# Down products of the first four inner tiles of the second feed-forward stage as products of halves

## The chip, the core and the metric

The kernel runs on one core of a Trainium2 chip. The time is that of the device, in microseconds (us), from the start of the program to its end on that core. The engines have names that the profile shortens: PE (TensorE, matrix products), PEld (its weight loads, beside PE), DVE (VectorE), ACT (ScalarE), POOL (GpSimd), SP (SyncE, which here only issues DMAs). SBUF is the on-chip memory, PSUM the accumulators that PE writes.

## The reference, cut to what matters

One decoder layer over 512 tokens of width 1024, all in 32-bit floats:

```python
def swiglu_ffn(x, g, w_gate, w_up, w_down):
    h = rms_norm(x, g)
    return (jax.nn.silu(h @ w_gate) * (h @ w_up)) @ w_down
...
x = x + 0.5 * swiglu_ffn(x, ffn1_norm, ffn1_w_gate, ffn1_w_up, ffn1_w_down)
...
x = x + 0.5 * swiglu_ffn(x, ffn2_norm, ffn2_w_gate, ffn2_w_up, ffn2_w_down)
```

Between the two lie two attention branches, which the change doesn't touch. The inner width of a feed-forward stage is 2816, which is 22 inner tiles of 128 (numbered f, from 0).

## The kernel before

**Layout.** x lies in SBUF as eight tiles of 128 features by 512 tokens (`x[d]`, all in one tile `gx`, which `xa` views). Products are computed with features on the partitions and tokens along the columns.

**Three products for one.** A 32-bit operand is split into a high part (rounded to the type that PE takes in one pass, `fp32r`) and a low part, the remainder. `mm3` (lines 155 to 157) issues high x high, low x high and high x low. The weights are split by `split_w` in the kernel: ACT casts the raw tile to `wh` (line 123), and DVE subtracts for `wl` (line 130), or, with `adding`, ACT negates and a DMA of POOL that adds in memory does the rest. `wh` and `wl` have three buffers each, so a step's weights can be split up to two steps ahead.

**Products of halves.** A product of two matrices cut in 2 x 2 blocks needs eight products of blocks; a known scheme (Strassen's, in Winograd's form) needs seven, with sums of blocks ahead of them and behind. The kernel uses it for most of a feed-forward stage. Tokens are cut in halves of 256 (`HT`). Of the weights, blocks A, B, C, D are loaded, and the sums S1 = C + D, S2 = S1 - A in the signs used, S2 + B and C + A are formed. Of the activations, the moving operands are `b1` and `b2` (halves as they are) and the sums `ta` and `tb`, each with high and low part. The order of the seven steps is 1, 5, 6, 2, 7, 3, 4, with moving operands b1 first half, ta first, tb first, b2 first, ta second, b2 second, tb second.

**Stages of `ffn(n, nxt)`.** `GROUPS` cuts the 22 inner tiles into (0,4), (4,10), (10,16), (16,22). In the first group everything is plain: for each of the four inner tiles a gate and an up step (24 products of 512 columns each, over the eight x tiles), then `activate` (DVE multiplies by the norm scale `rb`, ACT applies Silu, DVE multiplies gate and up; `split_act` splits the result); then eight down steps, one for each output tile d, by `run_down`, each with 12 products of 512 columns (four inner tiles, three terms). The first two put their last inner tile off behind both. In the other three groups the gate and up products of each pair of inner tiles are seven steps of halves (`pair_steps`, 24 products of 256 columns a step), and the down products of the group are two sets `s` of seven steps (`halved_steps(lo, s)`, each set for four output tiles, `GK` = 3 pairs, so 18 products of 256 columns a step).

**Beside the first group** of the second stage, `combine(k)` forms the operands of halves of x for the pair steps, for k of 0 to 3: the normalised x in a tile `xn` in buffer `rd` (line 336), then the sums (lines 340 to 343) and the splits (lines 328 and 329). Two pieces of it are emitted behind each step as soon as the norm scale is there, and behind the last one `rd` becomes free for raw weights.

**Order.** PE runs in program order throughout. `look_ahead(i)` splits the weights of step i and the next two, and issues loads up to six steps ahead while one of the raw buffers `ra`, `rb`, `rc`, `re`, `rf` (and later `rd`) is free; all these loads go through SP's queue. From `ordered[0]`, the first pair step, ACT, DVE and POOL also run in program order; ahead of it a scheduler orders them when the program is built, by program order as a priority and by its own estimate of when things are ready. On the chip that order is fixed.

Of the kernel before, what the change touches and what calls it, by code (L numbers as in the profile page):

```python
# [12 lines left out]
F32 = mybir.dt.float32  # L13
F32R = mybir.dt.float32r
AF = mybir.ActivationFunctionType
OP = mybir.AluOpType
# [32 lines left out]
HK = KD // 2  # L49
GK = 3  # L50
HALVED = (4, 10, 16)
FIRST = [0, 1, 4, 5, 2, 3, 6, 7]


@with_exitstack
def tile_hybrid_layer(ctx: ExitStack, tc: tile.TileContext, a: dict):
# [14 lines left out]
    def tmp_tile(name):  # L71
        return tmp.tile([P, T], F32, tag="t", name=name)
# [31 lines left out]
    def stream(i, dtype, name):  # L104

        return xpool.tile([P, 2 * T], dtype, tag=f"X{i}", name=name)
# [101 lines left out]
    def ffn(n, nxt):  # L208
# [3 lines left out]
        with tc.tile_pool(name=f"ffn{n}", bufs=1) as ap, tc.tile_pool(name=f"halves{n}", bufs=1) as hp:  # L212
# [21 lines left out]
            def halves(q):  # L234
                lo = next(lo for lo, hi in GROUPS if lo <= 2 * q < hi)
                j = q - lo // 2
                if q not in act:
                    tiles = [ap.tile([P, 2 * T], F32R, tag=f"a{j}{i}", name=f"a{i}") for i in "hl"]
                    ta = stream(6 + j, F32R, "ta") if j < 2 else ap.tile([P, 2 * T], F32R, tag="a2t", name="ta")
                    b1 = ap.tile([P, T], F32R, tag=f"a{j}b", name="b1")  # L240
                    act[q] = dict(b2=[t[:, :T] for t in tiles], tb=[t[:, T:] for t in tiles],
                                  ta=[ta[:, :T], ta[:, T:]], b1=[b1[:, :HT], b1[:, HT:]])
# [62 lines left out]
            def activate(f, pg, pu, rb):  # L305
                g = tmp_tile("g")
                V.tensor_mul(g, pg, rb)
                S.activation(g, g, AF.Silu)
                u = tmp_tile("u")
                V.tensor_mul(u, pu, rb)  # L310
                V.tensor_mul(u, u, g)
                split_act(f, u, 1 < f < PLAIN - 1)


            def parts_tile(nm, cols):
# [183 lines left out]
            def halved_steps(lo, s):  # L499

                t, raw = {}, {}
                n_w = 2 * GK * P
                end = lo + 2 * GK == KF
                direct = end and s and n == 2
                to_mix = end and n == 1

                def split(src, between=None):
                    return split_w(src, n_w, halves=True, between=between)
# [2 lines left out]
                    return lambda: V.tensor_add(dst[:, :n_w], x0[:, :n_w], x1[:, :n_w])  # L511

                def split_a():
                    t["s1"] = stream(0, F32, "s1")
                    return split(raw["a"][0], add(t["s1"], raw["c"][0], raw["d"][0]))

                def split_s1():
                    t["s2"] = stream(1, F32, "s2")
                    w = split(t["s1"], add(t["s2"], t["s1"], raw["a"][0]))
                    G.dma_start(raw["c"][0][:, :n_w], raw["a"][0][:, :n_w], accum_op=OP.add)  # L520
                    return w

# [1 line left out]
                    add(t["s2"], t["s2"], raw["b"][0])()  # L524

                def split_b():
                    if s:
                        return split(raw["b"][0], add_b)
                    w = split(raw["b"][0], late.pop("fa"))
                    late.pop("b2")()  # L530
                    add_b()
                    return w

                def split_s4():
                    if s:
# [7 lines left out]
                    return ps.rearrange("p (m t) -> p m t", m=2)  # L543

                def product(nm, w, b, half, start, each=None):
                    wh, wl = (z[:, :n_w].rearrange("p (m k c) -> p m k c", m=2, k=GK) for z in w)
                    order = [(m, k) for ks in (range(GK - 1), [GK - 1]) for m in range(2) for k in ks]
                    if each:
                        order.sort()
                    for i, (m, k) in enumerate(order):  # L550
                        h, l = (z[:, half * HT:half * HT + HT] for z in act[lo // 2 + k][b])
                        mm3(t[nm if each is None else nm + "01"[m]][:, m * HT:(m + 1) * HT], wh[:, m, k], wl[:, m, k], h, l,
                            start and i == 0, i == 2 * GK - 1 or (each is not None and k == GK - 1), skip_group_check=True)
                        if each and k == GK - 1:
                            each(m)

                def add_up(nm, part, half, done, sign=0.5, ms=(0, 1)):
# [67 lines left out]
                def run_4(w):  # L625
# [9 lines left out]
                return [Step(raw, [load["c"], load["d"], load["a"]], split_a, run_1),  # L635
                        Step(raw, [], split_s1, run_5),
                        Step(raw, [load["b"]], lambda: split(t["s2"]), run_6, "a"),
                        Step(raw, [], split_b, run_2, "b"),
                        Step(raw, [], lambda: split(raw["c"][0]), run_7, "c"),
                        Step(raw, [], split_s4, run_3),  # L640
                        Step(raw, [], lambda: split(raw["d"][0]), run_4, "d")]

            def run_down(d, lo, hi, held={}):

# [85 lines left out]
            def load():  # L730
                i, (key, f, src) = queue.pop(0)

                tag = max(sorted(free), key=lambda z: used[::-1].index(z) if z in used else len(used))
                free.remove(tag)
                used.append(tag)
                t = ap.tile([P, 1024], F32, tag=tag, name=tag) if tag in ("rd", "re", "rf") else raw_tile(tag)
                steps[i].raw[key] = t, tag
                nc.sync.dma_start(t[:, :f * P].rearrange("p (n m) -> p n m", n=f) if f else t, src)

            def look_ahead(i):  # L740

# [725 lines left out]
def _layout(x, ffn1_norm, ffn1_w_gate, ffn1_w_up, ffn1_w_down, mix_norm, w_in, b_forget,  # L1467
# [8 lines left out]
    for n, (g, u, dn) in ((1, (ffn1_w_gate, ffn1_w_up, ffn1_w_down)), (2, (ffn2_w_gate, ffn2_w_up, ffn2_w_down))):  # L1476
# [5 lines left out]
        o[f"w_down{n}"] = _fm(dn)  # L1482

        dh = _fm(dn)[:, :, PLAIN:].reshape(2, 2, 2, P, -1, GK, 2, P)
        o[f"w_halves{n}"] = dh.transpose(4, 1, 0, 6, 3, 2, 5, 7).reshape(-1, 2, 4, P, 2 * GK, P)
    c = lambda lo, hi: w_in[:, lo:hi]
    o["w_s"] = _tm(np.concatenate([c(2056, 2120), c(2696, 2760), c(2120, 2184), c(1536, 1544), c(2760, 2768)], axis=1))[:, FIRST]
# [32 lines left out]
```

## Time and profile before

| what | value |
|---|---|
| median of 3 runs | 1048.84 us (1047.35 to 1049.34) |
| the profiled execution, whole | 1048.76 us |
| its span | 1047.0 us |
| gate and up steps of the first group, second stage | about 719 to 763.4 us |
| its eight down steps | 763.4 to 785.1 us |
| pair steps and halved down steps behind it | 785.1 to 1047.0 us |

The span is the time between the first and the last record of the profiled execution; the rest of its own time lies around it. How to read the rows of the timeline: start in us, duration in us, engine, line of the kernel, operation, out<-in by the program's names, shapes, a count where equal instructions are merged, and in brackets the time that the engine sat idle before it with what ended that. The duration of an instruction is from its start to its end; instructions of one engine overlap a little, so the pace of a row of them is read from start to start.

DVE's work by stage, from the windows view (start and end, length; busy us and number of instructions of PE, PEld, DVE, ACT, POOL; granted TensorE clock; DMA share; GB/s):

```profile
719.00:763.40 44.40, 44.40 (x204) 36.86 (x203) 30.24 (x55) 25.07 (x38) 5.44 (x6) 1.00 0.46 107
763.40:785.10 21.70, 21.70 (x97) 17.98 (x96) 18.55 (x27) 7.54 (x12) 0.00 (x0) 1.00 0.55 175
785.10:804.00 18.90, 18.90 (x167) 18.88 (x166) 12.95 (x13) 9.87 (x12) 0.00 (x0) 1.00 0.29 93
```

### The profile page before, as it was taken

The page shows a single profiled execution, that of the slowest core. Times are in us where ns is not written, and L with a number is a line of the kernel's source. Part 1 is how long each engine was busy: PE and PEld are TensorE (multiplying, and loading weights), DVE is VectorE, ACT ScalarE, POOL GpSimd, SP SyncE. Part 2 cuts the span into 40 slices and gives each one's busy share as a digit, 9 for nine tenths or more (in the row PEclk, how much of TensorE's full clock was granted, in tenths as well). Part 3 has the DMA queues.
Part 4 walks back from the last instruction along what each step waited for, and adds up shares of the span by engine and source line. Part 5 has one row for each costly group of instructions (what it writes and reads, how often), then busy time and mean ns, then how long its engine had stood idle before and what let it go on. Part 6 is the DMA issues. An engine that isn't in the chain of part 4 may idle for free.

```text
span 1047.0 us, 19507 instructions
## 1 busy us (share of the span) xinstructions
PE 1036.7 (99%) x7438; PEld 965.7 (92%) x7438; DVE 852.4 (81%) x1402; ACT 669.0 (64%) x1118; POOL 257.7 (25%) x323
## 2 busy tenths in 40 slices
PE   9999999999999999999999999999999999999998
PEld 7889999999999899999977788888889999999998
DVE  6897888897989689977777865854887888988887
ACT  6547765865777765577867665443735865775773
POOL 1100111120121025286876653000100210111111
PEclk9999999999999999999999999999999999999999
DMA  7444764666567367633324321432553666567554
GB/s 256 107 151 122 156 165 131 149 164 172 120 149 181 87 149 182 197 98 95 92 66 120 118 71 51 154 132 77 129 168 91 151 148 182 126 161 189 135 127 131
DMA packets 57341, 142.66 MB, mean 136 GB/s; under 512 B 6424, under 2 KB 15768, under 8 KB 57248
## 3 DMA queue, kind: packets, MB, share of 16 engines
q1 hardware_dynamic: 39600, 110.21, 34.3%
q0 software_dynamic: 17504, 30.94, 16.5%
q8 instruction: 58, 0.95, 0.4%
q10 hardware_dynamic: 144, 0.27, 0.1%
q14 instruction: 35, 0.29, 0.1%
HBM read 104.94 MB, written 3.42 MB: 103 GB/s over the span
## 4 chain that ended last, share of the span: by engine, by line
PE 69%; DVE 3%; POOL 2%; issue 2%; ACT 1%; DMA 0%; POOLq 0%; ACTq 0%; DVEq 0%
PE pB L155 3%; PE pB L157 3%; PE pB L156 3%; PE ps_f L155 3%; PE ps_f L157 3%; PE ps_f L156 3%; PE ps_t L157 3%; PE ps_t L155 3%; PE ps_t L156 3%; PE pA L155 2%; PE pA L156 2%; PE pA L157 2%; PE dB L155 2%; PE dB L157 2%; PE dB L156 2%
## 5 line engine op out<-in xcount | busy, mean ns | idle before, releaser
L123 ACT CAST wh<-s 128x1024 fp32r<-128x1024 f32 (+1 forms) x90 | 86.7, 964 | 65.7 <-PE pC L156 31.6
L130 DVE TENSOR_TENSOR wl<-s,wh 128x1024 fp32r<-128x1024 f32 (+1 forms) x90 | 100.3, 1114 | 19.9 <-ACT wh L123 19.6
L155 PE MATMUL ps_t<-wh,xh 128*128 128x256 f32 (+1 forms) x288 | 81.9, 284 | 0.0
L157 PE MATMUL ps_t<-wh,xl 128*128 128x256 f32 (+1 forms) x288 | 81.2, 282 | 0.2 <-DVE xl L168 0.2
L156 PE MATMUL ps_t<-wl,xh 128*128 128x256 f32 (+1 forms) x288 | 81.0, 281 | 0.0
L155 PE MATMUL pB<-tbh,wh 128*128 128x256 f32 x288 | 79.5, 276 | 0.0
L156 PE MATMUL pB<-tbl,wh 128*128 128x256 f32 x288 | 79.5, 276 | 0.0
L157 PE MATMUL pB<-tbh,wl 128*128 128x256 f32 x288 | 79.5, 276 | 0.0
L249 POOL DMA_DIRECT2D b<-gu x12 | 10.4, 863 | 220.4 <-DVE rb L449 89.4
L155 PE MATMUL ps_f<-xh,wh 128*128 128x512 f32 x152 | 60.8, 400 | 0.0
L157 PE MATMUL ps_f<-xh,wl 128*128 128x512 f32 x152 | 59.6, 392 | 0.0
L156 PE MATMUL ps_f<-xl,wh 128*128 128x512 f32 x152 | 59.5, 392 | 0.0
L155 PEld LDWEIGHTS ps_t<-wh,xh 128*128 128x128 f32 x288 | 54.8, 190 | 0.4
L156 PEld LDWEIGHTS ps_t<-wl,xh 128*128 128x128 f32 x288 | 54.7, 190 | 0.4
L157 PEld LDWEIGHTS ps_t<-wh,xl 128*128 128x128 f32 x288 | 54.6, 190 | 0.4 <-DVE xl L168 0.4
L1237 ACT ACTIVATE p<-p,mn 128x512 f32<-128x512 f32 (+1 forms) x64 | 35.9, 561 | 28.5 <-DVE mn L1235 28.2
L157 PEld LDWEIGHTS pB<-tbh,wl 128*128 128x128 f32 x288 | 54.1, 188 | 0.0
L156 PEld LDWEIGHTS pB<-tbl,wh 128*128 128x128 f32 x288 | 54.1, 188 | 0.0
L155 PEld LDWEIGHTS pB<-tbh,wh 128*128 128x128 f32 x288 | 54.1, 188 | 0.0
L575 POOL DMA_DIRECT2D gx<-e x20 | 23.9, 1241 | 119.9 <-ACT wh L123 100.4
L1239 POOL TENSOR_SCALAR p<-p,rs 128x512 f32<-128x512 f32 (+1 forms) x64 | 39.6, 622 | 54.5 <-DVE rs L1238 50.3
L1251 DVE TENSOR_TENSOR pl<-pt,ph 128x512 fp32r<-128x512 f32 (+1 forms) x64 | 31.0, 485 | 19.4 <-ACT ph L1250 19.3
(404 smaller groups left out, 4195.3 us busy)
## 6 DMA issues: line engine op xcount, KB each, us to landing
rf<-in_w_pair_dram SPq DMA_DIRECT2D x15, 512.0 KB, 4.1
rc<-in_w_pair_dram SPq DMA_DIRECT2D x12, 512.0 KB, 3.5
re<-in_w_pair_dram SPq DMA_DIRECT2D x12, 512.0 KB, 3.7
rd<-in_w_pair_dram SPq DMA_DIRECT2D x12, 512.0 KB, 3.9
rb<-in_w_pair_dram SPq DMA_DIRECT2D x12, 512.0 KB, 4.2
gx<-e POOLq DMA_DIRECT2D x22, 256.0 KB, 4.3
ra<-in_w_pair_dram SPq DMA_DIRECT2D x9, 512.0 KB, 3.6
rd<-in_w_halves_dram SPq DMA_DIRECT2D x12, 384.0 KB, 3.8
```

The lines of the kernel that those rows point to most:

```text
L123: S.copy(wh[:, :f], raw[:, :f])
L130: V.tensor_sub(wl[:, :f], raw[:, :f], wh[:, :f].bitcast(F32))
L155: PE.matmul(out, lh, rh, start=start, stop=False, **more)
L156: PE.matmul(out, lh, rl, start=False, stop=False, **more)
L157: PE.matmul(out, ll, rh, start=False, stop=stop, **more)
L249: G.dma_start(l, src, accum_op=OP.add)
L575: G.dma_start(xa[:, d:d + 2, HT:], t["e"][part], accum_op=OP.add)
L1237: S.activation(p, p, AF.Exp, bias=mn, scale=-1.0, accum_out=rs)
L1239: G.tensor_scalar(p, p, rs, 1.0, op0=OP.mult, op1=OP.mult)
L1251: V.tensor_sub(pl[:, sl], pt[:, sl], ph[:, sl].bitcast(F32))
```

## The change

In the second stage alone (`FRONT = (2,)`) the eight plain down steps of the first group become two sets of `halved_steps(0, s)`, with two pairs of inner tiles in place of three, so 12 products of 256 columns a step. `activate` no longer ends in `split_act` but in a new function, `front_act`, which forms `b1`, `b2`, `ta`, `tb` from the inner tiles of a pair; for the last tile it does the two token halves one after the other. `sums_at` places `ta`: for the first pair in the tile `a2t`, for the second in buffer X7 of x's split, once the last gate and up products have read that. The weights come in a new layout `w_front` as three loads of 512 KB for each set, two blocks in one load: "ss" (one that becomes S1, and one that S2 is added into), "cd", "ab". S1 is formed by an accumulating DMA of POOL, in place of an addition by DVE. With `ordered[1] = -1` the kernel's order rules for the pair steps stay as they were.

```diff
+            def sums_at(q, home):
+                ta = (ap.tile([P, 2 * T], F32R, tag=home, name="ta") if home == "a2t" else stream(home, F32R, "ta"))
+                act[q]["ta"] = [ta[:, :T], ta[:, T:]]
...
                 S.activation(g, g, AF.Silu)
+                if n in FRONT:
+                    return front_act(f, g, pu, rb)
                 u = tmp_tile("u")
...
+            def front_act(f, g, pu, rb):
+                q, last = f // 2, f == PLAIN - 1
+                t = halves(q)
+                first, second, both = slice(0, HT), slice(HT, T), slice(0, T)
+                if f % 2 == 0:
+                    kept_u = ap.tile([P, 2 * T], F32, tag="a2" + "hl"[q], name="u1")
+                    u, fa = t["u1"], t["fa"] = kept_u[:, :T], kept_u[:, T:]
+                    V.tensor_mul(u, pu, rb)
+                    V.tensor_mul(u, u, g)
+                    V.tensor_sub(fa[:, first], u[:, first], u[:, second])
+                    split_late(q, "b1", u[:, first], first)
+                    return
+                if last:
+                    sums_at(q, 7)
+                    high_low(q, "ta", t["fa"], first)
+                u, fb, u1, fa = tmp_tile("u"), tmp_tile("fb"), t["u1"], t["fa"]
+                for h in (second, first) if last else (both,):
+                    V.tensor_mul(u[:, h], pu[:, h], rb[:, h])
+                    V.tensor_mul(u[:, h], u[:, h], g[:, h])
+                    if h != first:
+                        V.scalar_tensor_tensor(fb[:, first], fa[:, first], -1.0, u[:, second], op0=OP.mult, op1=OP.subtract)
+                    if last and h == second:
+                        high_low(q, "tb", fb, first)
+                V.tensor_sub(fa[:, second], u[:, second], u1[:, second])
+                V.scalar_tensor_tensor(fb[:, second], fb[:, first], -1.0, u[:, first], op0=OP.mult, op1=OP.subtract)
+                if last:
+                    high_low(q, "b2", u, both)
+                    high_low(q, "ta", fa, second)
+                    high_low(q, "tb", fb, second)
+                else:
+                    high_low(q, "ta", fa, both)
+                    split_late(q, "b2", u, both)
+                    high_low(q, "tb", fb, both)
...
-                n_w = 2 * GK * P
-                end = lo + 2 * GK == KF
+                gk = GK if lo else PLAIN // 2
+                n_w = 2 * gk * P
+                end = lo + 2 * gk == KF
...
                 def split_a():
+                    if lo == 0:
+                        (ss, tag), (ab, _), (cd, _) = (raw[z] for z in ("ss", "ab", "cd"))
+                        t["s1"], t["s2"], raw["a"], raw["b"], raw["c"], raw["d"] = ss[:, :n_w], ss[:, n_w:], *(
+                            (w[:, i * n_w:(i + 1) * n_w], None) for w in (ab, cd) for i in range(2))
+                        G.dma_start(t["s1"], raw["d"][0], accum_op=OP.add)
+                        return split(raw["a"][0])
...
                 def split_s1():
-                    t["s2"] = stream(1, F32, "s2")
-                    w = split(t["s1"], add(t["s2"], t["s1"], raw["a"][0]))
+                    if lo:
+                        t["s2"] = stream(1, F32, "s2")
+                        w = split(t["s1"], add(t["s2"], t["s1"], raw["a"][0]))
+                    else:
+                        w = split(t["s1"])
+                        V.tensor_add(t["s2"], t["s2"], t["s1"])
                     G.dma_start(raw["c"][0][:, :n_w], raw["a"][0][:, :n_w], accum_op=OP.add)
...
-                load = {z: (z, 2 * GK, wh_[(lo - PLAIN) // (2 * GK), s, i]) for i, z in enumerate("abcd")}
+                if lo == 0:
+                    front = a[f"w_front{n}"][s].rearrange("z p c -> p z c")
+                    loads = ([("ss", 2, front[:, 0:2]), ("cd", 2, front[:, 0::3]), ("ab", 2, front[:, 1:3])], [])
+                    frees = "", ("ab",), (), ("ss",), ("cd",)
...
+                if n in FRONT:
+                    for s in range(2):
+                        steps += halved_steps(lo, s)
+                    ordered[1] = -1
+                    continue
```

The rest of the change passes `gk` and the new names through `halved_steps`, lets the load of two blocks into `load`, and adds `w_front` to the layout of the inputs.

More of the change, by code (lines that the diff above doesn't have):

```diff
@@ L51 @@
 HALVED = (4, 10, 16)
+FRONT = (2,)
 FIRST = [0, 1, 4, 5, 2, 3, 6, 7]
@@ L238, in halves @@
                     tiles = [ap.tile([P, 2 * T], F32R, tag=f"a{j}{i}", name=f"a{i}") for i in "hl"]
-                    ta = stream(6 + j, F32R, "ta") if j < 2 else ap.tile([P, 2 * T], F32R, tag="a2t", name="ta")
                     b1 = ap.tile([P, T], F32R, tag=f"a{j}b", name="b1")
-                    act[q] = dict(b2=[t[:, :T] for t in tiles], tb=[t[:, T:] for t in tiles],
-                                  ta=[ta[:, :T], ta[:, T:]], b1=[b1[:, :HT], b1[:, HT:]])
+                    act[q] = dict(b2=[t[:, :T] for t in tiles], tb=[t[:, T:] for t in tiles], b1=[b1[:, :HT], b1[:, HT:]])
+                    if q != 1:
+                        sums_at(q, "a2t" if lo == 0 or j == 2 else 6 + j)
                 return act[q]
+            def sums_at(q, home):
+                ta = (ap.tile([P, 2 * T], F32R, tag=home, name="ta") if home == "a2t" else stream(home, F32R, "ta"))
+                act[q]["ta"] = [ta[:, :T], ta[:, T:]]
             def split_late(q, nm, src, cols):
@@ L545, in product @@
                 def product(nm, w, b, half, start, each=None):
-                    wh, wl = (z[:, :n_w].rearrange("p (m k c) -> p m k c", m=2, k=GK) for z in w)
-                    order = [(m, k) for ks in (range(GK - 1), [GK - 1]) for m in range(2) for k in ks]
+                    wh, wl = (z[:, :n_w].rearrange("p (m k c) -> p m k c", m=2, k=gk) for z in w)
+                    order = [(m, k) for ks in (range(gk - 1), [gk - 1]) for m in range(2) for k in ks]
                     if each:
@@ L552, in product @@
                         mm3(t[nm if each is None else nm + "01"[m]][:, m * HT:(m + 1) * HT], wh[:, m, k], wl[:, m, k], h, l,
-                            start and i == 0, i == 2 * GK - 1 or (each is not None and k == GK - 1), skip_group_check=True)
-                        if each and k == GK - 1:
+                            start and i == 0, i == 2 * gk - 1 or (each is not None and k == gk - 1), skip_group_check=True)
+                        if each and k == gk - 1:
                             each(m)
@@ L632, in run_4 @@
                         finished(1)
-                load = {z: (z, 2 * GK, wh_[(lo - PLAIN) // (2 * GK), s, i]) for i, z in enumerate("abcd")}
-                return [Step(raw, [load["c"], load["d"], load["a"]], split_a, run_1),
-                        Step(raw, [], split_s1, run_5),
[L637 to L641, printed above, removed]
+                if lo == 0:
+                    front = a[f"w_front{n}"][s].rearrange("z p c -> p z c")
+                    loads = ([("ss", 2, front[:, 0:2]), ("cd", 2, front[:, 0::3]), ("ab", 2, front[:, 1:3])], [])
+                    frees = "", ("ab",), (), ("ss",), ("cd",)
+                else:
+                    load = {z: (z, 2 * GK, wh_[(lo - PLAIN) // (2 * GK), s, i]) for i, z in enumerate("abcd")}
+                    loads = [load["c"], load["d"], load["a"]], [load["b"]]
+                    frees = "abc" + " d"
+                return [Step(raw, loads[0], split_a, run_1),
+                        Step(raw, [], split_s1, run_5),
+                        Step(raw, loads[1], lambda: split(t["s2"]), run_6, frees[0]),
+                        Step(raw, [], split_b, run_2, frees[1]),
+                        Step(raw, [], lambda: split(raw["c"][0]), run_7, frees[2]),
+                        Step(raw, [], split_s4, run_3, frees[3].strip() if lo else frees[3]),
+                        Step(raw, [], lambda: split(raw["d"][0]), run_4, frees[4])]
             def run_down(d, lo, hi, held={}):
@@ L737, in load @@
                 steps[i].raw[key] = t, tag
-                nc.sync.dma_start(t[:, :f * P].rearrange("p (n m) -> p n m", n=f) if f else t, src)
+                nc.sync.dma_start(t.rearrange("p (n m) -> p n m", n=f) if f == 2 else
+                                  t[:, :f * P].rearrange("p (n m) -> p n m", n=f) if f else t, src)
             def look_ahead(i):
```

6 lines of the change are left out of this document (4 added, 2 removed).

## The prediction

> **What bounds the kernel now.** I read the page's busy shares first, then the view of waits of PE (TensorE) over the second feed-forward stage (from 700 us), which lists none, then the windows view, then the timelines of PE, DVE (VectorE) and the DMA queues. The page, and the windows (span stretch, its length, then busy us and instructions of PE, PEld, DVE, ACT, POOL, then granted clock, DMA share, GB/s):
>
> ```profile
> PE 1036.7 (99%) x7438; PEld 965.7 (92%) x7438; DVE 852.4 (81%) x1402; ACT 669.0 (64%) x1118; POOL 257.7 (25%) x323
> ...
> 735.00:785.10 50.10, 50.10 (x222) 41.49 (x221) 44.57 (x76) 27.54 (x43) 3.47 (x4) 1.00 0.56 148
> 844.00:860.00 16.00, 16.00 (x141) 16.00 (x142) 15.93 (x25) 10.93 (x19) 3.32 (x3) 1.00 0.59 150
> 840.00:880.00 40.00, 40.00 (x353) 39.84 (x352) 36.85 (x48) 24.67 (x38) 5.72 (x5) 1.00 0.65 166
> ```
>
> TensorE is never idle around the change, at a granted clock of 1.00: it sets the end, and a microsecond taken from it or waited by it moves the end by as much. VectorE comes next: 44.57 of the 50.10 us from the norm scale to the last down product, so only 5.53 us free. From 844 to 860 us lies the stage's own first set of seven products of halves (groups of three pairs): there VectorE is busy 15.93 of 16.00 us and TensorE still waits for nothing. That is the form which the change brings in, with less TensorE work per step to hide behind.
>
> **What it removes and adds on TensorE.** Removed are eight down steps of 12 products of 512 columns, added 2 x 7 steps of 12 products (two output tiles, two pairs, three terms) of 256 columns.
>
> ```profile
> 763.36 0.39 PE L155 MATMUL pd<-ah,wh 128*128 128x512 f32 x1
> ...
> 784.89 0.39 PE L157 MATMUL pd<-ah,wl 128*128 128x512 f32 x1
> 785.11 0.28 PE L155 MATMUL pA<-b1h,wh 128*128 128x256 f32 x1
> ...
> 787.94 0.28 PE L155 MATMUL pD<-tah,wh 128*128 128x256 f32 x1
> ```
>
> The 96 old products run from 763.36 to 785.11: 21.75 us, 0.227 each start to start. A product of 256 columns takes 40.00/353 = 0.113 us (840 to 880); the 24 from 785.11 to 787.94 took 0.118. So the 168 new ones cost 19.04 us, 19.8 at the slow pace; I take 19.04, the pace of hundreds. TensorE by itself **saves 2.71 us**, and the first pair product would start at 763.36 + 19.04 = 782.40. One new step is 1.36 us.
>
> **What it adds on VectorE.** The pace, start to start, from one unbroken row of instructions:
>
> ```profile
> 734.97 0.69 DVE L197 COPY rb<-ps_rb 128x512 f32<-128x512 f32 x1 [3.16 <-PE ps_rb L195]
> ...
> 739.15 0.69 DVE L311 TENSOR_TENSOR u<-u,g 128x512 f32<-128x512 f32 x1 [0.85 <-ACT g L308]
> ...
> 750.12 0.42 DVE L343 SCALAR_TENSOR_TENSOR tb<-tb,xn 128x256 f32<-128x256 f32 x1
> 750.45 0.69 DVE L329 TENSOR_TENSOR tal<-ta,tah 128x512 fp32r<-128x512 f32 x1
> 751.05 1.41 DVE L336 SCALAR_TENSOR_TENSOR xn<-gx,rb 128x512 f32<-128x512 f32 x2
> 752.38 0.69 DVE L329 TENSOR_TENSOR tbl<-tb,tbh 128x512 fp32r<-128x512 f32 x1
> 752.98 0.42 DVE L329 TENSOR_TENSOR b1l<-xn,b1h 128x256 fp32r<-128x256 f32 x1
> ...
> 776.90 1.22 DVE L446 TENSOR_TENSOR s<-s,rd 128x1024 f32<-128x1024 f32 x1
> 778.04 1.22 DVE L449 TENSOR_TENSOR rb<-rb,rd 128x1024 f32<-128x1024 f32 x1
> 779.17 0.68 DVE L666 SCALAR_TENSOR_TENSOR gx<-pd,gx 128x512 f32<-128x512 f32 x1
> ```
>
> So 512 columns cost 0.60 us, 256 cost 0.335, 1024 cost 1.14; the two of `xn` 1.33 together. Behind 734.97, until the weights of the first pair product are split, VectorE must now do: the norm scale (one of 512); tile 0, three of 512 and one of 256; tile 1, five and three (two lows, and the three sums); tile 2, three and one; tile 3, two of 512 and eleven of 256, as its two halves go apart; `combine`, 20 and 20; 14 weight splits; the two S2 sums of each set, 4; six of the eight additions into x (the last two may come later); and for the pair step S1 and one split, two of 1024. That is 58 x 0.60 + 0.5 (the slower `xn`) + 36 x 0.335 + 2 x 1.14 = **49.6 us**. The S1 sums of the two sets and C + A go to POOL's accumulating DMAs and cost VectorE nothing.
>
> With the 0.85 us in which it waits for the first Silu (that stays), VectorE is done at 734.97 + 49.6 + 0.85 = 785.4, against 782.40 for TensorE alone and 785.11 before. One step on it is tighter: the next pair step (787.94 before) needs the two put-off additions, S2 and its split as well, 1.2 + 2 x 1.14 = 3.5 us, so 788.9: **0.96 us later than before**, with VectorE never idle. Two steps further the same count gives 0.5, then 0.1 us. So the 2.71 us are spent on waiting for VectorE, and 1.0 more.
>
> The old 1.62 us of idle ahead of tile 3's up product (row below) is filled, since the new work ahead of it is 2.9 us (0.335 in tile 0, 1.6 in tile 1, 0.335 in tile 2, S2 0.6). For other idle time of a VectorE that runs in a fixed order, the ends are nothing (844 to 860: 0.07 us in 16) and 5.53 - 0.85 = 4.7 (as before, when it was not the bound); I take 0.7, near the first, since it will be behind as there. **Sum: 0.96 + 0.7 = 1.7 us slower.**
>
> [...] With the durations my 49.6 would be an estimated 57.9.
>
> **What else it moves.** ACT gains six weight copies, four copies and four evictions from PSUM, and some 2.4 us of highs: about 10 us on 27.54 of 50.10, covered. On POOL eleven DMA issues are added (two S1, two C + A, four additions of evicted products, three lows, against one before) at 0.85 us, on 3.47 us of 50.10, covered; what waits behind a POOL DMA is other accumulation, and a `wl` of the gate and up steps early on, which have two steps of 5.4 us. On SP's queue eight loads of 256 KB become six of 512 KB.
>
> ```profile
> 758.09 0.85 POOL L230 DMA_DIRECT2D al<-u  x1 [6.80 <-ACT al L229]
> ...
> 763.56 0.69 DVE L310 TENSOR_TENSOR u<-pu,rb 128x512 f32<-128x512 f32 x1 [1.62 <-PE pu L157]
> ...
> 766.97 0.42 DVE L343 SCALAR_TENSOR_TENSOR tb<-tb,xn 128x256 f32<-128x256 f32 x1
> ...
> 767.42 0.33 SPq L738 DMA_DIRECT2D rd<-in_w_pair_dram  x1
> ...
> rd<-in_w_pair_dram SPq DMA_DIRECT2D x12, 512.0 KB, 3.9
> rd<-rf POOLq DMA_DIRECT2D x3, 384.0 KB, 4.7
> ```
>
> The new wait is behind tile 3. Before, its first use came after 18 products (4.1 us); now after two steps and half of the third (3.4 us), and `tb`, `b2`, second `ta` and `tb` must follow at 1.36 us each, while VectorE does 4.9 us of that tile. If TensorE stops there, it is the same VectorE time that is counted above, not another cost.
>
> **The rivals.**
>
> *It gains.* The scheduler need not keep program order ahead of the pair steps. If it puts the eight additions into x (0.6 each) behind the splits of the pair steps, up to 3.6 us leave the count at the tightest step, and the end is set by TensorE alone at best: 1048.76 - 2.71 = 1046.05; with 2.1 us put off it is 1048.76 + 0.96 - 2.1, about 1047.6. Against it: before, such additions came as soon as their product ended (779.17, between two sums), and the accumulators that they free are needed three allocations on.
>
> *The second set's A comes late (slower).* Its A and B weights go to buffer `rd`, which `combine` holds until its last L343; the row of SP shows that load 0.03 us behind that instruction. Landing takes 3.9 us, copy and split 0.62 + 0.69. Before, L343 ended at 767.39; with 1.3 us of new backlog and about 1 us of tile 3 ahead I put it at 769.4, so A is split at 774.6. Its step would start at 763.36 + 7 x 1.36 = 772.9, and by then some 2 to 3 us of the waits have gone by: hidden. It decides from an L343 end of about 770.5: all of tile 3 and two splits ahead of it would make it 773, the step 2.5 to 3 us late, in which VectorE has nothing to do: 1050.5 + 3 = 1053.5. C + A of that set (4.7 us by DMA) hangs on the same load.
>
> *Full durations.* If VectorE's small instructions did not overlap, 57.9 + 0.85 us put the first pair product at 793.7, 8.6 us late: 1057.4. The rows show overlap everywhere, so this has little. [...]
>
> *It doesn't do what it says*, in that the 256-column products keep the 0.118 us: 0.8 us less is saved on TensorE, which is waiting anyway, so about the forecast; or VectorE's count is too high by over 2 us, and it gains.
>
> **How the numbers follow.** The profiled execution took 1048.76 us, 1047.0 of it span; the median of the runs is 1048.84, so 0.08 more: the same. Forecast 1048.76 + 1.7 = **1050.5 us**, between 1049.0 and 1052.4 for 0 to 3.5 us of idle time; chance 0.52. The gain 0.25, the late load 0.16, full durations 0.02, not as said 0.05. The range goes from 1046.6 (most of TensorE's saving) to 1053.8 (the late load); the cases of both signs are that close. About 0.2%, 2.1 us, is what a measurement of this kernel can tell from no change: below 1046.7 lies three fifths of the gain and a part of the last case, 0.17; above 1050.9 two fifths of the forecast, the late load and the durations, 0.38; between them 0.45.
>
> **What would show it.** Right: 168 products of 256 columns in place of 96 of 512 at 0.113 us; idle time of PE of 3 to 6 us between the end of tile 3's up product and the third pair step, released by DVE (`wl`, or a low of tile 3); VectorE over 95% busy in that stretch; the first pair product near 786. Wrong: no such idle time (then the first pair product starts near 782.4 and the count of VectorE is too high), or PE released by ACT or by `rd`'s load (then the late load), or VectorE with more than 3 us idle while PE waits.

## The result, and the profile after

The changed kernel takes 1061.86 us (median of 4 runs, 1059.77 to 1063.08), the kernel before 1048.3 in the same session: a ratio of 1.0124, 95% interval 1.0112 to 1.0137, so 13.6 us slower. The forecast was 1050.5.

The profiled execution of the changed kernel took 1063.08 us, its span is 1061.4. First its view of waits of PE in the second feed-forward stage (tile waited with, line, engine and tile that released it; us in total, times, longest). Before, that view was empty. Behind `halves`, `mm3` is now L156 to 158.

```profile
PE pu L158 <- DMA wl<-rc: 3.0, 1, 3.0
PE dA L157 <- DMA b<-u: 2.0, 1, 2.0
PE dB L156 <- ACT ah L257: 1.7, 1, 1.7
PE dB L157 <- DVE al L261: 1.3, 1, 1.3
PE dA L158 <- DVE wl L131: 1.2, 1, 1.2
PE dD L157 <- DVE ta L261: 0.9, 1, 0.9
```

PE waits 10.1 us, half of that for DMAs, which the forecast had called covered. Then the windows view from the norm scale to the first down product (767.98), from there to the first pair product (799.96), and over both, with a finer cut for the clock below (columns as before: PE, PEld, DVE, ACT, POOL, granted clock, DMA share, GB/s):

```profile
736.30:767.98 31.68, 28.72 (x126) 23.38 (x125) 25.46 (x50) 20.40 (x33) 7.23 (x9) 1.00 0.67 152
767.98:799.96 31.98, 24.90 (x169) 23.61 (x168) 27.99 (x49) 17.23 (x31) 5.04 (x5) 0.79 0.51 136
736.30:799.96 63.66, 53.62 (x294) 46.99 (x293) 53.45 (x99) 37.63 (x64) 12.27 (x13) 0.89 0.59 144
...
772.00:784.00 12.00, 8.12 (x35) 7.24 (x34) 11.58 (x27) 7.72 (x16) 0.86 (x1) 0.50 0.27 66
```

From the norm scale to the first pair product it was 50.14 us (734.97 to 785.11); now it is **63.66**, and these 13.5 us are nearly the whole loss. I call this length *the stretch*; it doesn't depend on where an execution's span starts. VectorE is busy 53.45 us in it (44.6 before) and idle 9.9. Its timeline shows where (idle time and releaser in brackets):

```profile
763.42 0.42 DVE L385 SCALAR_TENSOR_TENSOR tb<-tb,xn 128x256 f32<-128x256 f32 x1
770.18 0.69 DVE L572 TENSOR_TENSOR rb<-rb 128x512 f32<-128x512 f32 x1 [6.34 <-DMA rb<-rc]
770.79 1.41 DVE L378 SCALAR_TENSOR_TENSOR xn<-gx,rb 128x512 f32<-128x512 f32 x2
772.12 0.68 DVE L371 TENSOR_TENSOR tbl<-tb,tbh 128x512 fp32r<-128x512 f32 x1
772.72 0.42 DVE L371 TENSOR_TENSOR b1l<-xn,b1h 128x256 fp32r<-128x256 f32 x1
773.05 0.75 DVE L339 TENSOR_TENSOR u<-pu,rb 128x256 f32<-128x256 f32 x2
```

L572 is `V.tensor_add(t["s2"], t["s2"], t["s1"])` of the **second** front set; that S2 is first used in the tenth of the fourteen front steps. The scheduler put it ahead of tile 3 (L339) in VectorE's queue. It waits 6.34 us for the S1 DMA, and the k = 3 operands (L378) and all of tile 3 stand behind it. The timelines of POOL and of SP's queue say why that DMA is late:

```profile
754.43 0.85 POOL L573 DMA_DIRECT2D rf<-ra  x1 [7.50 <-DVE ta L261]
754.97 1.20 POOL L254 DMA_DIRECT2D al<-u  x1
755.51 1.55 POOL L129 DMA_DIRECT2D wl<-rc  x1
766.90 0.86 POOL L561 DMA_DIRECT2D rb<-rc  x1 [9.85 <-DMA rc<-in_w_front_dram]
767.44 1.21 POOL L254 DMA_DIRECT2D b<-u  x1
```

```profile
752.37 0.37 SPq L803 DMA_DIRECT2D rb<-in_w_front_dram  x1
762.83 0.37 SPq L803 DMA_DIRECT2D rc<-in_w_front_dram  x1
```

The C and D weights of the second set go to `rc`, which still holds the raw up weights of tile 3. Those are read by an accumulating DMA (`wl<-rc`, issued 755.51), and the next load into `rc` is issued at 762.83, when PE too starts on that `wl` after its 3.0 us. Then the load, then the S1 DMA, then S2. `b<-u` of tile 2, issued right behind the S1 DMA on POOL, is the other DMA that PE waits for.

### The profile page after: what moved, and what is told of

Read it like the earlier page. It is cut to its first block, busy times and chain, and to the rows that moved or that the text cites. A ratio compares the mean times of both kernels' runs of the same rounds, so it can differ in the third digit from the quotient of the medians.

```text
span 1061.4 us, 19730 instructions
## 1 busy us (share of the span) xinstructions
PE 1041.3 (98%) x7510; PEld 972.6 (92%) x7510; DVE 862.2 (81%) x1426; ACT 679.3 (64%) x1140; POOL 267.6 (25%) x333
## 4 chain that ended last, share of the span: by engine, by line
PE 89%; DVE 4%; DMA 3%; ACT 2%; issue 1%; POOL 1%; POOLq 0%; DVEq 0%; SPq 0%
PE pB L156 5%; PE pB L157 5%; PE pB L158 5%; PE ps_f L156 3%; PE ps_f L157 3%; PE ps_f L158 3%; PE pA L156 3%; PE pA L157 3%; PE pA L158 3%; PE ps_t L156 3%; PE ps_t L158 3%; PE ps_t L157 3%; PE dB L158 3%; PE dB L157 3%; PE dB L156 3%; PE dA L157 2%
## 5 line engine op out<-in xcount | busy, mean ns | idle before, releaser
L156 PE MATMUL ps_t<-wh,xh 128*128 128x256 f32 (+1 forms) x288 | 81.8, 284 | 0.0
L156 PE MATMUL pB<-tbh,wh 128*128 128x256 f32 x288 | 79.5, 276 | 0.0
L628 POOL DMA_DIRECT2D gx<-e x24 | 28.8, 1250 | 134.6 <-ACT wh L124 99.3
L156 PE MATMUL ps_f<-xh,wh 128*128 128x512 f32 x152 | 60.8, 400 | 0.0
L156 PEld LDWEIGHTS ps_t<-wh,xh 128*128 128x128 f32 x288 | 54.8, 190 | 0.4
L156 PEld LDWEIGHTS pB<-tbh,wh 128*128 128x128 f32 x288 | 54.1, 188 | 0.0
```

What stands on the lines that cost most here:

```text
L156: PE.matmul(out, lh, rh, start=start, stop=False, **more)
L628: G.dma_start(xa[:, d:d + 2, HT:], t["e"][part], accum_op=OP.add)
```

## The experiments

Eighteen more kernels ran, beside the kernel before and the changed one. The table gives, from each profiled execution, the stretch, VectorE's busy time in it (windows view) and the sum of its bracketed idle times (timeline); then the median and its ratio to before. Busy and idle add up to the stretch by definition, within 0.6 us, so the split alone proves no cause; the runs do that. A profile is of one execution: in f1, c1 and k4 that execution was 1.9, 2.1 and 3.2 us faster than the median, in f4 2.0 us slower, in the others at most 1.2 us off.

| run | stretch | busy | idle | us | ratio, 95% interval |
|---|---|---|---|---|---|
| before | 50.14 | 44.6 | 5.0 | 1047.3 to 1048.7 | 1 |
| changed kernel | 63.66 | 53.5 | 9.9 | 1061.86 | 1.0124 [1.0112, 1.0137] |
| e1_in_order | 62.26 | 50.2 | 12.0 | 1060.34 | 1.0121 [1.0106, 1.0136] |
| e2_up3_low_by_vector | 61.15 | 55.7 | 5.2 | 1059.32 | 1.0111 [1.0095, 1.0126] |
| e3_three_mends | 62.57 | 52.4 | 10.0 | 1061.22 | 1.0134 [1.0116, 1.0153] |
| e4_no_low_weights | 59.65 | 44.9 | 14.7 | 1057.2 | 1.0091 [1.0076, 1.0106] |
| h1_by_deadline | 64.03 | 51.6 | 12.2 | 1061.47 | 1.0135 [1.012, 1.0151] |
| h2_pool_order | 60.59 | 53.6 | 6.6 | 1058.19 | 1.0101 [1.0086, 1.0116] |
| h4_operands_ahead | 64.09 | 52.0 | 11.7 | 1062.91 | 1.0136 [1.0117, 1.0155] |
| c1_filled_waits | 63.09 | 53.0 | 9.9 | 1064.5 | 1.016 [1.0144, 1.0175] |
| f1_no_tail | 61.65 | 53.0 | 8.7 | 1060.82 | 1.0114 [1.0099, 1.0129] |
| f2_no_front_dma | 62.83 | 52.8 | 9.6 | 1061.47 | 1.012 [1.0103, 1.0137] |
| f3_no_tail_no_dma | 62.43 | 52.4 | 9.9 | 1060.38 | 1.0115 [1.0099, 1.013] |
| f4_no_tail_dma_low | 55.13 | 44.4 | 10.5 | 1052.26 | 1.004 [1.0025, 1.0055] |
| k1_no_second_s2 | 61.11 | 53.0 | 7.7 | 1058.91 | 1.0104 [1.0084, 1.0125] |
| k2_no_tail_dma_low_s2 | 48.53 | 43.5 | 4.9 | 1046.03 | 0.998 [0.9969, 0.9992] |
| k3_s1_by_vector_in_order | 59.67 | 50.7 | 8.9 | 1057.96 | 1.0085 [1.007, 1.01] |
| k4_same_no_low | 53.28 | 42.5 | 10.5 | 1054.97 | 1.0061 [1.0044, 1.0077] |
| l1_low_weights_back | 54.23 | 52.0 | 2.1 | 1051.73 | 1.003 [1.0017, 1.0042] |
| l2_tail_back | 49.69 | 43.4 | 6.3 | 1047.65 | 0.9994 [0.9984, 1.0004] |

### The first theory: waits behind the heads of queues and behind tile 3

The first theory (queue theory) was that work which is ready stands in queues behind instructions that wait for a DMA. Its rival (capacity theory) was that VectorE simply has too much to do, in whatever order.

**e1_in_order.** Program order for ACT, VectorE and POOL from the first front set on:

```diff
                 if n in FRONT:
+                    ordered[0] = len(steps)
                     for s in range(2):
```

> The changed kernel, but from the first step of halves of the first group on ACT, DVE and POOL run in program order (as they do from the pair steps on), so the second set's S1 DMA and S2 sum stand behind tile 3's work. Queue theory (instructions that wait for a DMA stand ahead of work that is ready): the 6.3 us of VectorE idle before the S2 sum and the 2.0 us of PE waiting for b go, with most of the 3.9 us of waits on tile 3 and the half clock behind them (some 4 us); the 3.0 us for the up step's low weights stay: about 1052 us. Capacity theory (VectorE has too much to do): VectorE's work is the same, so 1059 us or more.

PE's wait for `b` and VectorE's wait at the S2 sum went, and the time hardly moved (1060.34). In program order the second S1 DMA is issued late (780.04), and the split of its weights now has VectorE idle ahead of it, as its timeline shows:

```profile
786.04 0.69 DVE L131 TENSOR_TENSOR wl<-rb,wh 128x512 fp32r<-128x512 f32 x1 [6.09 <-ACT wh L124]
```

**e2_up3_low_by_vector.** The low weights of tile 3's gate and up steps are formed by VectorE, not by POOL's DMA:

```diff
-  plain(w[f - skip], KD, run(f), f > 1)
+  plain(w[f - skip], KD, run(f), f > 1 and (f < 3 or n not in FRONT))
```

> The changed kernel, but the low weights of tile 3's gate and up steps are formed by VectorE in place of POOL's accumulating DMA (two more of 1024 columns, 2.3 us). Queue theory: the 3.0 us of PE waiting for these weights go, and the raw buffer rc comes free some 5 us sooner, so the second set's loads and S1 do too and the 6.3 us idle of VectorE shrinks below 2: about 1051 us. Capacity theory: 2.3 us more on VectorE, at best no change, 1061 to 1064 us.

This cures what it should: `rc` is free early (the split that reads it ends at 751.94), L572 waits 0.57 us instead of 6.34, no PE wait is left for a DMA, and VectorE's idle time falls from 9.9 to 5.2. But it brings VectorE two more splits of 1024 columns (2.3 us); busy 55.7, and the stretch is still 61.15. This run speaks for VectorE's sum of work.

**e3_three_mends.** Both of these, and the load of "ab" goes to `rd` where that is free (`if key == "ab" and "rd" in free: tag = "rd"`).

> Both edits, program order and tile 3's low weights by VectorE, and the second set's A and B loaded to rd rather than to ra. Queue theory: no PE wait on a DMA is left; what remains is the wait for VectorE of the forecast, 1049 to 1052 us at full clock. Capacity theory: 1058 us or more.

1061.22: nothing. The late second S1 DMA of e1 is back.

**e4_no_low_weights.** The 14 low weights of the front sets are left out (`split_w` returns `wh` for `wl`).

> The changed kernel with the 14 low weights of the two sets left out (the high part stands in for the low one in the products, so TensorE's work is the same): 8.4 us less on VectorE in the stretch, the order of the rest as it was. Capacity theory: the 4 to 5 us of PE waiting for VectorE go, and with them the half clock: 1053 us or less. Queue theory: the waits for DMA stay (3.0 and 2.0 us, and VectorE's 6.3 us), and so do most waits on tile 3: 1058 to 1061 us.

8.4 us less VectorE work gave 4.7 us; VectorE's idle time grew from 9.9 to 14.7, of which 7.32 at the same S2 sum. Of these four runs the capacity theory had e1 and e3 right; e2 and e4 fell into the range of neither theory.

**h2, h4, h1** set the order by hand. h2: POOL alone in program order, with the S1 DMAs issued earlier by place:

```diff
+                if n in FRONT and i in (4, 10):
+                    r = steps[8 if i == 4 else 15].raw
+                    G.dma_start(r["ss"][0][:, :T], r["cd"][0][:, T:], accum_op=OP.add)
```

> The changed kernel with POOL alone in program order and the S1 DMAs moved as in h1; VectorE's and ACT's order stay with the scheduler. If POOL's queue is the cause: no PE wait on a DMA is left (3.0 and 2.0 us in the changed kernel), and no wait of VectorE for an S1 DMA (6.3 us), 1050 to 1053 us. If VectorE's order is: the waits on tile 3 stay at 5 us or more, 1054 to 1058 us, still with the half clock.

h4: that, program order for ACT and VectorE from tile 3's up step on, and tile 3's second halves put off behind the B and S4 weights (as the later groups do with `late`).

> h1, but with the operands of k = 3 of the pair steps (4.8 us of VectorE) left where the change has them, ahead of tile 3's sums. Order theory: they stand in the way of tile 3 for up to 4.8 us of PE waiting, 3 to 5 us slower than h1. Capacity theory: the same work in total, within 1 us of h1.

h1: that, and the k = 3 operands put behind the first five front steps (`if rbs and combos and not (n in FRONT and 7 <= i < 12)`).

> The changed kernel with its order placed by hand: POOL in program order through the whole second stage, the S1 DMAs of the two sets issued once nothing ready stands behind them; from tile 3's up step on ACT and DVE in program order, with tile 3's second half, b2 and the last sums issued between the weight splits (as the later groups do it), and the operands of k = 3 of the pair steps behind the first set. Order theory (what PE waits for behind tile 3 is ready late only because of what the queues hold ahead of it): the waits fall below 3 us, the clock stays at 1.00, 1047 to 1050 us. Capacity theory (VectorE's total work in the stretch sets the end whatever the order): 1049 to 1052 us, with VectorE over 95% busy between tile 3 and the first pair step. DMA theory (the accumulating DMAs and the second set's loads are too late in any order): a wait of 3 us or more at the second set, 1052 us or more.

h2 gave 3.7 us against the changed kernel, a little less than either of its ranges. h4 and h1 can't be told apart (1.4 us, with intervals that overlap), so the place of the k = 3 operands decided nothing here. In h1 no wait of PE for an operand of tile 3 is left, and yet it takes 1061.47, more than 9 us over what both the order and the capacity theory gave it: its stretch has VectorE idle 3.80 and 3.19 us behind weight casts and 2.74 behind tile 3's `ta`. Each order that I wrote freed one wait and exposed another.

**c1_filled_waits.** 51 products of 256 columns into an unused accumulator, placed in the waits of the first front set, so that PE isn't idle there and its clock stays up:

```diff
+                        if lo == 0 and s == 0 and k and not m and (nm, b, half) in FILLED:
...
+                            for _ in range(FILLED[nm, b, half]):
+                                PE.matmul(act["idle"][:, :HT], wh[:, 0, 0], act[0]["b1"][0], start=True, stop=True)
```

> The changed kernel with 51 more products of 256 columns (17, 8 and 26, to a bank that nobody reads) where PE waits in the first three steps of the first set, 5.8 us at full clock. If the half clock from 772 to 785 us comes of PE's idle time there: the clock stays at 1.00 and the time falls by up to 4 us, to 1058 to 1060 us. If not: half clock again, and 1062 us or more, since the added products then take longer than the waits.

The granted clock stayed at 1.00, where the changed kernel had 0.50 from 772 to 784: here it was PE's idle time that had brought it down (5.9 us of 764 to 784 in the changed kernel, 2.4 us in c1). And yet nothing was won; neither expectation came true as a whole:

```profile
735.76:798.85 63.09, 55.58 (x345) 49.07 (x344) 52.99 (x99) 37.42 (x64) 12.31 (x13) 1.00 0.62 148
```

Against the changed kernel's row, the granted clock is 1.00 instead of 0.89 and the stretch 63.09 instead of 63.66. This speaks for the half clock as a symptom: VectorE's work isn't done sooner when PE runs faster to the next wait. It is no clean proof, since the 51 products take time of their own (5.8 us at 0.113 each), and the median is 2.6 us higher with them.

### The first theory falls

Four runs were to sum it up. f1: products of the second pair read the first pair's operands (`act[lo // 2 + (k if lo else 0)]`). f2: the front sets' S1 and C + A DMAs left out. f3: both. f4: both, and no low weights.

> The products of the front sets that read the second pair (tiles 2 and 3) read the first pair's operands instead, so no down product depends on tile 3; all work on VectorE, ACT and POOL is still done. Theory (each step waits for a chain of its own: tile 3's sums and casts, and the accumulating DMAs that stand ahead in the queues): tile 3's part of the waits (b, ah, al, ta: 5.9 of 10.1 us) goes, the rest stays, and with less idle time some of the half clock (4.1 us) goes too: about 1054 (1052 to 1057) where the changed kernel is 1061. Rival (VectorE's sum of work is what decides, wherever it stands): its work is the same, so 1060 to 1062.

> Leaves out the accumulating DMAs that form S1 and C + A in the two front sets. Theory of chains and queues: the wait for the low weights of the up product (3.0 us) goes, since nothing stands ahead of that DMA, and tile 3's low by DMA is no longer behind S1 (part of 2.0 us); the casts and sums of tile 3 remain: 1057 (1055 to 1059). Rival (VectorE's sum alone): VectorE's work is the same: 1060 to 1062.

> Both of the two above. Theory of chains and queues: what is left is the split of weights at 1.36 us a step, so 1048 to 1051, with PE's waits under 3 us and the clock at 1.00 but for a few us. Rival (VectorE's sum alone): still 1060 to 1062, as VectorE has the same work.

> The two above and, as in the run without low weights, the 14 splits of low weights of the front sets left out (their products use the high weights twice). Nothing that the theory names is left between TensorE and its 168 products, so the saving of 2.7 us should show: 1045 to 1048, PE's waits under 1 us and the clock at 1.00. If it stays over 1050, a cause is missing from the theory.

f1 to f3 stayed at 1060.4 to 1061.5, where the theory wanted 1048 to 1059: with no product that depends on tile 3's late operands and no accumulating DMA of the front sets, the stretch is still 62.4 us. The rival, VectorE's sum of work, had 1060 to 1062 for all three and was right. Only f4 moved, to 1052.26, and even that is 1.004 of before. The windows and the timeline of VectorE in f3 show what stayed:

```profile
735.75:798.18 62.43, 52.74 (x294) 46.22 (x293) 52.42 (x98) 37.52 (x64) 8.77 (x9) 0.92 0.56 135
```

```profile
752.25 0.42 DVE L385 SCALAR_TENSOR_TENSOR tb<-tb,xn 128x256 f32<-128x256 f32 x1
759.68 0.69 DVE L571 TENSOR_TENSOR rb<-rb 128x512 f32<-128x512 f32 x1 [7.01 <-issue]
```

The second set's S2 sum again. Without the S1 DMA it stands even earlier in the queue and waits for the load of `rb`: in f4, whose idle time at this place is 6.82 us, that load was issued at 752.50, took 7.0 us to land, and the sum began at 759.63.

```profile
752.50 0.37 SPq L803 DMA_DIRECT2D rb<-in_w_front_dram  x1
...
rb<-in_w_front_dram SPq DMA_DIRECT2D x1, 512.0 KB, 7.0
```

```profile
759.63 0.69 DVE L571 TENSOR_TENSOR rb<-rb 128x512 f32<-128x512 f32 x1 [6.82 <-issue]
```

No product of f4 reads tile 3's operands, and still the idle time reaches PE, by way of ACT. ACT waits 7.62 us for VectorE's `xn`, and the copy of an accumulator that PE needs for its third step (`dB<-dA`, L638) stands behind these casts in ACT's queue. It starts 6.4 us after the first down product (764.28), and PE waits 3.96 us for it:

```profile
761.62 0.41 ACT L370 CAST b1h<-xn 128x256 fp32r<-128x256 f32 x1 [7.62 <-DVE xn L378]
...
770.70 0.58 ACT L638 COPY dB<-dA 128x512 f32<-128x512 f32 x1
```

```profile
771.33 0.44 PE L156 MATMUL dB<-ah,wh 128*128 128x256 f32 x1 [3.96 <-ACT dB L638]
```

**The new theory:** VectorE's work is the bound, as forecast, and on top of it VectorE stands idle for 6 to 7 us behind one sum that is not needed yet; PE's waits for tile 3 and for weights are mostly the same lateness seen from PE.

### The second theory

**k1** and **k2** leave the second set's S2 sum out (`if s == 0:` ahead of L572), k1 in the changed kernel, k2 in f4.

> Leaves out one instruction, the S2 sum of the second front set (0.60 us of VectorE). Theory (the stretch from the norm scale to the first pair product is VectorE's busy plus its idle time): busy 52.9, and of 9.9 us idle 6.3 go, some of it back since the up product of tile 3 still waits 3 us for its low weights: 57 to 59 us where it was 63.7, so 1055 to 1058. Rival (each step waits on a chain behind tile 3, wherever VectorE idled before): 1059 to 1061.

> The run without tile 3's chain, front DMAs and low weights (1052.3, stretch 55.1 us), with the second set's S2 sum left out too. Theory: busy 43.8 plus 3.5 to 5 of idle, so TensorE's own 28.4 + 19.0 = 47.4 us decide: 1046 to 1048, under before. Rival (a cause is still missing): over 1050.

k2 is f4 without one instruction of 0.6 us. In VectorE's queue over this stretch the only other difference is one `g` product two places on. ACT's copy `dB<-dA` starts 1.6 us after the first down product (764.33 and 762.71), not 6.4. k2 is 6.2 us faster, 1046.03, a ratio of 0.998 [0.9969, 0.9992] to before, and PE has one wait left:

```profile
734.32:782.85 48.53, 47.78 (x295) 42.66 (x293) 43.53 (x83) 37.24 (x64) 8.80 (x9) 1.00 0.68 174
```

```profile
PE dB L156 <- ACT dC L656: 0.7, 1, 0.7
```

So the list of causes is enough: with all of them gone TensorE's saving shows. k1 just misses its range: the stretch fell from 63.66 to 61.11 and the time to 1058.91 (1055 to 1058 expected, 1059 to 1061 by the rival). With the DMAs and tile 3's chain still there, those hold PE and then VectorE, which is idle in five pieces of 1.0 to 1.6 us, four of them new, in place of one of 6.3. This looks like two covers that lie over each other, each hiding most of the other.

**l1** and **l2** put one thing each back into k2.

> As the run at 1046.0 (without tile 3's chain, front DMAs, low weights, second S2 sum), with the 14 low weights put back: 8.4 us more of VectorE. If VectorE's sum is a bound of its own: busy 52 plus 2.5 to 4 of idle, so a stretch of 54.5 to 56 us and 1052.5 to 1054.5. If the idle time and the chains made all of the loss: under 1049.

> As the run at 1046.0, with tile 3's chain put back (its products read their own operands); no low weights, no front DMAs, no second S2 sum. VectorE has 43.5 us of work and nothing foreign ahead of tile 3 but the k = 3 operands: waits of PE for b, ah, al of 1 to 4 us, so 1046.5 to 1050. Over 1051 tile 3's chain would be a bound of its own.

```profile
734.10:788.33 54.23, 50.70 (x295) 44.75 (x293) 51.99 (x98) 37.50 (x64) 8.81 (x10) 0.97 0.59 144
```

l1: VectorE busy 51.99 of 54.23 us, idle 2.1, and the kernel takes 1.003 [1.0017, 1.0042] of before. That is the forecast's mechanism alone: VectorE's sum, with hardly any idle time. (At 1051.73 it is a little under what was expected of it.) l2: tile 3's chain costs 1.2 us of stretch (49.69) when nothing else is late, and the time is the same as before.

**k3** computes everything: program order as in e1, and S1 of the second set as a sum on VectorE (`if s: return split(raw["a"][0], add(t["s1"], t["s1"], raw["d"][0]))`), so that no DMA stands ahead of it. **k4** is k3 without the low weights.

> The whole computation: program order from the first front set, and S1 of the second front set by VectorE (0.60 us) in place of the accumulating DMA. Against the run in program order (stretch 62.3 us, busy 50.2, idle 12.0 of which 6.1 behind that DMA): busy 51, idle 5.5 to 7: 56.5 to 58 us, so 1054.5 to 1057. Rival (chains): 1059 to 1061.

> The one above with the 14 low weights of the front sets left out (8.4 us of VectorE). Theory: busy 42.5, so TensorE's 47.4 us and a little waiting decide, 47.5 to 50: 1046 to 1049. Rival (chains): 1055 to 1057, as the run without low weights alone.

k3, at 1057.96, is the fastest of the kernels that do the whole computation, but still 1.0085 of before. It and k4 (1054.97) both miss their ranges upwards: the stretch was 59.67 and 53.28 where 56.5 to 58 and 47.5 to 50 were expected. k4's trace flatters it: its execution took 1051.76, the other three 1054.8 to 1055.4. The two largest pieces of k3's 8.9 us of idle time are 2.94 us in which VectorE waits for tile 3's up product, and 2.77 behind the cast of the second set's C + A:

```profile
766.79 0.76 DVE L339 TENSOR_TENSOR u<-pu,rb 128x256 f32<-128x256 f32 x2 [2.94 <-PE pu L158]
...
788.48 0.69 DVE L131 TENSOR_TENSOR wl<-rc,wh 128x512 fp32r<-128x512 f32 x1 [2.77 <-ACT wh L124]
```

The first is behind the accumulating DMA of `wl<-rc` (PE waits 2.4 us for it here), the second behind the C + A DMA, which POOL issues at 782.75, after two additions of evicted products in its program order. So the accumulating DMAs, and what stands ahead of them, still hold VectorE once the second S1 no longer comes by DMA. Their price by themselves isn't shown: no run puts them alone back into k2.

The nearest kernel that does the whole computation, k3, is 9.5 us slower than the one before.

## Why the prediction was wrong

The sum of the forecast put the stretch at 51.1 us (first pair product 0.7 behind 785.4); it was 63.66, so 12.5 us were missed. VectorE's extra idle time is 8.3 of them and its extra work 3.9.

- **The step that failed:** "For other idle time of a VectorE that runs in a fixed order, the ends are nothing ... and 5.53 - 0.85 = 4.7 ...; I take 0.7, near the first, since it will be behind as there." Measured: 9.9 - 0.85 = 9.0 us, more than either end. The reason given was wrong: VectorE was behind in work and still stood idle when the head of its queue wasn't ready. In the sets from which I took the 0.07 us (844 to 860) VectorE forms S1 itself, in program order; in the front sets S1 comes from a DMA behind a load, and a scheduler placed the sum that needs it. That one sum is the largest piece, 6.34 of the 9.9 us. Where the other late things were gone, taking it out shortened the stretch by 6.6 us (f4 to k2) and 8.2 us (f3 to l1, where the scheduler also set some dozen other instructions of VectorE in another order); where they were left in, by 2.6 (k1).
- **What fed it:** "On POOL eleven DMA issues are added ..., covered." I compared POOL's issue time with the stretch, not the chain of each DMA: `wl<-rc` holds `rc`, `rc` holds back the load, the load the S1 DMA, that the S2 sum, and the sum VectorE. `wl<-rc` itself was issued 2.5 us after ACT had its operand ready (753.01), behind the first set's C + A DMA and `al<-u` in POOL's queue (rows above), and PE waited 3.0 us for it, though the forecast gave such a `wl` two steps of 5.4 us. "The S1 sums ... go to POOL's accumulating DMAs and cost VectorE nothing" holds for work and not for waiting: k3, where VectorE does the second S1, beats e1 by 2.6 us of stretch.
- **VectorE's work**, put at 49.6 us, was 53.5. Of this, 2.3 are the pair step's S2 and C + A (791.62 and 792.75, 1.13 us each below), which stand ahead of the split of its first weights (798.41). I had put S2 one step later and left C + A out, though the quoted rows of before show both ahead of the first pair product (776.90, 778.04). A seventh addition into x (799.55) is the third instruction more than forecast: 59 of 512 columns, 36 of 256 and 4 of 1024 stand in the stretch where I had 58, 36 and 2. At the forecast's prices these are 52.5 us, so the prices held and the count was short.

```profile
791.62 1.22 DVE L488 TENSOR_TENSOR s<-s,rd 128x1024 f32<-128x1024 f32 x1
792.75 1.22 DVE L491 TENSOR_TENSOR re<-re,rd 128x1024 f32<-128x1024 f32 x1
...
798.41 1.23 DVE L131 TENSOR_TENSOR wl<-rd,wh 128x1024 fp32r<-128x1024 f32 x1
```

- **TensorE's saving** held but for 0.3 us: in k2 the 168 products take 20.14 us (first of them to first pair product) with 0.75 idle, so 0.115 us each, and the saving is 21.75 - 19.39 = 2.4 us where 2.71 was forecast.
- **VectorE as the bound that eats the saving** held as a mechanism: l1, which has almost no idle time, comes to 1.003 of before. It explains 3 of the 13.6 us.
- **The wait behind tile 3 as "the same VectorE time that is counted above, not another cost"**: nearly right. Taking its chain away alone gave 1 us (f1), and putting it back into k2 cost 1.2 us of stretch.
- **The late second set** was a rival, by way of `rd`. `combine` was done only at 781.96, far behind the 770.5 from which the rival reckoned, but the load of "ab" didn't go to `rd`: it went to `ra` (777.29), and PE began the second set (788.90) without a wait. It was the "cd" load and the S1 DMA that came late. The rival had the right set, the wrong buffer, and a price of 3 us for what cost 2.6 to 8.2 us of stretch.
- **Full durations**: no. At the durations of the rows of before (0.69 us for 512 columns, 0.42 for 256, 1.22 for 1024, 1.41 for the two of `xn`) the forecast's count comes to 57.7 us, near its 57.9. But behind one another the small instructions kept their pace, 0.335 us for 256 columns with a duration of 0.41 each, in the changed kernel's row of them:

```profile
777.73 0.41 DVE L342 SCALAR_TENSOR_TENSOR fb<-u,u 128x256 f32<-128x256 f32 x1
778.07 0.41 DVE L345 TENSOR_TENSOR u<-u,u 128x256 f32<-128x256 f32 x1
778.40 0.41 DVE L382 TENSOR_TENSOR ta<-xn 128x256 f32<-128x256 f32 x1
```

- **What would show it:** of the signs for "right", idle time of 3 to 6 us released by DVE, VectorE over 95% busy and 786 for the first pair product, none came: 10.1 us released by DMAs, DVE and ACT, 84% (53.45 of 63.66), and 799.96. "VectorE with more than 3 us idle while PE waits" was the right sign for wrong, and it came.

- **The range** "between 1049.0 and 1052.4 for 0 to 3.5 us of idle time" doesn't follow from the forecast's own sum: 1048.76 + 0.96 with 0 to 3.5 us added is 1049.7 to 1053.2. Either range lies far under 1061.86.

What stays open: how the 2.6 us of k1 and the 8.2 of f3 to l1 would divide the S2 sum's share in the changed kernel itself, since the covers lie over each other; what the accumulating DMAs cost by themselves; and whether an order exists in which the whole computation reaches l1's 1.003.

## What to carry to other kernels

When a change makes an engine the bound, don't only add up its work: go through its queue in order and ask of each new instruction which load or DMA makes it ready, which buffer that load waits for, and who still reads that buffer. A sum that is needed only steps later can hold up all that is needed next (6.34 us here), and an off-path DMA engine is "covered" only if no in-order queue waits for it. When cures made one at a time give nothing, take all suspects out at once until the gain shows, and then put them back one by one; here that showed what the runs with partial cures had not.

## What the runs showed of the hardware

TensorE's clock fell to 0.50 after short waits, and stayed at 1.00 where most of these were filled with products (c1, the row of 735.76 above). In the changed kernel PE was idle 2.96 us ahead of 762.82 and 1.99 us ahead of 770.95, and from about 771.7 to 785.3 the granted clock was 0.50 (the row of 772 to 784 above), back at 1.00 some 4.8 us after the last of PE's waits had ended (780.48); at 0.50, products of 256 columns went at 0.213 us each instead of 0.113:

```profile
770.95 0.39 PE L157 MATMUL dA<-b,wh 128*128 128x256 f32 x1 [1.99 <-DMA b<-u]
...
772.03 0.41 PE L158 MATMUL dD<-ta,wl 128*128 128x256 f32 x1
772.25 0.41 PE L156 MATMUL dD<-ta,wh 128*128 128x256 f32 x1
772.46 0.41 PE L157 MATMUL dD<-ta,wh 128*128 128x256 f32 x1
```

How much idle time it takes isn't shown: in k4 PE was idle 4.6 us of its stretch, 2.04 at the longest, and the granted clock stayed at 1.00. For TensorE alone, some 41 products at 0.213 us instead of 0.113 are an estimated 4 us; in this kernel c1 won nothing back by avoiding them, which fits a VectorE that was the later one.

The source of an accumulating DMA stayed taken until it had landed: the next load into `rc` was issued only 7.3 us after `wl<-rc` (755.51 to 762.83), which took 7.3 us to land, when PE's wait for that `wl` ended (762.82). In k3, where `wl<-rc` was issued at 753.15, PE started on that `wl` at 759.89 and the load followed at 759.90.
